# A row maximum over 64 MiB: the helper path for six rows goes, the loads are cut anew, and the first load comes as two transfers

## The chip, the cores and the metric

The kernel runs on one core of a Trainium2 chip. The metric is device time in microseconds (us) of one execution. Before the change three runs took 168.21, 168.44 and 169.49 us; the median is 168.44. One further view is the profile of one execution, whose span runs from its first to its last instruction.

## The reference

The input is float32 of shape 32 x 512 x 1024, drawn from a normal distribution; the output is the largest of the last 1024 elements:

```python
def reference(x):
    return np.max(x, axis=-1).astype(np.float32)
```

So there are 16,384 rows of 4,096 bytes, 67.1 MB to be read, and 64 KB to be written.

## The kernel before

The rows are laid over 128 partitions, 128 rows in each. They come in two blocks: 112 rows per partition, then 16. In a block, partition p holds consecutive rows of the input, so that a load of n rows per partition reads n x 4,096 consecutive bytes for each partition. `BLOCKS` lists the loads, as (n, m, w): n rows per partition are loaded, m of them go the helper path, and the result of these is folded in after load number w.

All loads are issued by SyncE (SP), in the order of the list, at L113. Their destination is a ring of 46 slots of 4,096 bytes per partition; a load takes n neighbouring slots and starts again at slot 0 where it would not fit. A load that takes used slots waits until the instructions that read them are done. The framework hands the loads eight semaphores in turn, so an issue can also wait for the landing of the load eight places back.

VectorE takes each load with one `reduce_max` (L124), which writes one value per row and partition into `res`. The last row of each partition is loaded as two halves (L134 into the ring, L135 into `tail`), reduced by L136 and L137; L137 takes the first half's result along with the second half.

Six rows per partition go another way (`by_gpsimd`): TensorE turns each row's 1024 columns in eight blocks of 128 x 128 into PSUM (L75), ScalarE copies them to SBUF (L81), GpSimd takes the maximum over the partitions (L83), TensorE turns one partition of that back in eight pieces of 128 x 1 (L88), and VectorE reduces the eight values per row (L95). `in_turn` holds the instructions of TensorE and of VectorE in the order in which they are written. The identity for the turns is made by GpSimd behind the first load (L121).

ScalarE issues two stores: the first block's results behind the last whole-row reduction (L140), the second block's at the end (L142).

## Time and profile before

| What | us |
|---|---|
| median of three runs | 168.44 |
| the profiled execution's own time | 169.49 |
| its span | 166.9 |
| VectorE (DVE) busy | 132.6 |
| TensorE (PE) busy | 16.6 |
| GpSimd (POOL) busy | 20.2 |
| ScalarE (ACT) busy | 7.4 |
| VectorE waits for loads, in total | 28.3 |
| VectorE waits for the turned-back rows (L95) | 3.5 |

In the profile, the slices are 40 equal parts of the span; a digit is the busy share in tenths. DVE is VectorE, DMA the mean share of the 16 transfer engines, and GB/s what they moved, counted where a packet starts. A line of the timeline has the start, the length, engine, line and operation, and in brackets how long the engine stood idle before and for whom. A row of the groups has the number of instructions, the total busy time, the mean length of one in ns, and the idle time ahead of them with what ended it. A row of the stretches has from and to, the length, each engine's busy time and count, the granted TensorE clock, the transfer engines' share and GB/s.

### The profile page before, as it was taken

What the parts mean: (1) busy time and instruction counts of PE and PEld (TensorE: products, weight loads), DVE (VectorE), ACT (ScalarE), POOL (GpSimd) and SP (SyncE); (2) the same over time, 40 slices, a digit from 0 to 9 for tenths busy, and PEclk for the clock granted to TensorE, in tenths of its full rate; (3) what the DMA queues carried; (4) which work ended last, traced back from release to release, by engine and by line L of the source; (5) the groups of instructions that cost most, each with busy time, mean ns of one, the idle gap of its engine ahead of it and who ended that gap; (6) DMA issues with size and microseconds to landing.
All of it is one profiled execution on the core that took longest, in us unless ns stands there. A gap on an engine that the chain in (4) does not pass through costs nothing.

```text
span 166.9 us, 329 instructions
## 1 busy us (share of the span) xinstructions
PE 16.6 (10%) x96; PEld 14.8 (9%) x96; DVE 132.6 (79%) x26; ACT 7.4 (4%) x7; POOL 20.2 (12%) x13
## 2 busy tenths in 40 slices
PE   0000000000000000000000000000008125382520
PEld 0000000000000000000000000000007125272420
DVE  0000089993999599986999999999999999999914
ACT  3000000000000000000000000000003100420200
POOL 0000000000000000000000000000002930777250
PEclk9999999999999999999999999999999855855555
DMA  6999879999979999989989999989999899999900
GB/s 236 471 471 471 383 324 471 471 471 412 442 324 471 471 457 427 442 348 495 412 389 415 433 512 400 464 384 442 461 389 440 385 457 404 418 405 411 392 15 16
DMA packets 3456, 67.18 MB, mean 403 GB/s; under 512 B 640, under 2 KB 640, under 8 KB 1792
## 3 DMA queue, kind: packets, MB, share of 16 engines
q1 hardware_dynamic: 3168, 67.11, 94.3%
q10 hardware_dynamic: 288, 0.07, 0.2%
HBM read 67.11 MB, written 0.07 MB: 403 GB/s over the span
## 4 chain that ended last, share of the span: by engine, by line
DMA 56%; DVE 29%; POOL 4%; PE 4%; issue 3%; POOLq 2%; ACT 1%; SPq 0%; ACTq 0%
DMA ring<-in_x_dram 56%; DVE res L124 28%; POOL top L83 4%; PE ps L75 2%; POOLq L168 2%; ACT sb L81 1%; PE back L88 1%; DVE res L137 0%; DVE tail L136 0%; SPq L113 0%; DVE res L95 0%; ACTq L81 0%
## 5 line engine op out<-in xcount | busy, mean ns | idle before, releaser
L124 DVE TENSOR_REDUCE res<-ring 128x1 f32<-128x1024 f32 (+7 forms) x20 | 131.3, 6599 | 28.4 <-DMA ring<-in_x_dram 28.3
L83 POOL PARTITION_ALL_REDUCE top<-sb x6 | 19.3, 3254 | 108.9 <-ACT sb L81 108.9
L75 PE MATMUL ps<-ident,ring 128*128 128x128 f32 x48 | 11.0, 418 | 129.1 <-DMA ring<-in_x_dram 129.1
L75 PEld LDWEIGHTS ps<-ident,ring 128*128 128x128 f32 x48 | 9.6, 224 | 129.1 <-issue 125.2
L81 ACT COPY sb<-ps 128x1024 f32<-128x1024 f32 x6 | 6.1, 1012 | 149.5 <-PE ps L75 149.5
L88 PE MATMUL back<-ident,top 1*128 1x1 f32 x48 | 5.7, 235 | 16.3 <-POOL top L83 16.3
L88 PEld LDWEIGHTS back<-ident,top 1*128 1x128 f32 x48 | 5.2, 201 | 17.9 <-POOL top L83 17.9
L95 DVE TENSOR_REDUCE res<-back 128x2 f32<-128x16 f32 (+1 forms) x4 | 0.6, 162 | 3.5 <-PE back L88 3.5
L121 POOL COPY ident<-ring 128x1 f32<-128x1 f32 x1 | 0.2, 188 | 21.1 <-DMA ring<-in_x_dram 21.1
masks.py:199 POOL TENSOR_SCALAR_AFFINE_SELECT ident<-ident 128x128 f32<-128x128 f32 x1 | 0.3, 282 | 10.5 <-issue 10.5
L81 ACT ACT_TABLE_LOAD x1 | 1.3, 1283 | 0.7 <-PEq L157 0.7
L137 DVE TENSOR_REDUCE res<-tail 128x1 f32<-128x513 f32 x1 | 0.7, 687 | 0.0
L136 DVE TENSOR_REDUCE tail<-ring 128x1 f32<-128x512 f32 x1 | 0.7, 674 | 0.0
masks.py:197 POOL MEMSET ident<- 128x128 f32 x1 | 0.2, 204 | 0.1
L157 POOL MEMSET const-float32-0.0<- 128x1 f32 x1 | 0.1, 98 | 0.2 <-issue 0.2
L157 POOL MEMSET const-uint8-127<- 128x1 uint8 x1 | 0.1, 102 | 0.0
L157 POOL MEMSET const-bfloat16-1.0<- 128x1 bf16 x1 | 0.1, 101 | 0.0
L157 POOL MEMSET const-float32-1.0<- 128x1 f32 x1 | 0.1, 98 | 0.0
## 6 DMA issues: line engine op xcount, KB each, us to landing
ring<-in_x_dram SPq DMA_DIRECT2D x4, 7680.0 KB, 39.0
ring<-in_x_dram SPq DMA_DIRECT2D x2, 3584.0 KB, 26.5
ring<-in_x_dram SPq DMA_DIRECT2D x1, 6144.0 KB, 34.7
ring<-in_x_dram SPq DMA_DIRECT2D x1, 5632.0 KB, 37.9
ring<-in_x_dram SPq DMA_DIRECT2D x1, 5120.0 KB, 32.3
ring<-in_x_dram SPq DMA_DIRECT2D x7, 512.0 KB, 21.1
ring<-in_x_dram SPq DMA_DIRECT2D x1, 2560.0 KB, 33.7
ring<-in_x_dram SPq DMA_DIRECT2D x1, 2048.0 KB, 38.1
```

What stands on the lines that cost most here:

```text
L75: in_turn("PE", nc.tensor.transpose(out=ps[:, c * P:(c + 1) * P], in_=rows[:, k, c * P:(c + 1) * P], identity=ident,))
L81: nc.scalar.copy(out=sb, in_=ps)
L83: nc.gpsimd.partition_all_reduce(top, sb, P, bass_isa.ReduceOp.max)
L88: in_turn("PE", nc.tensor.transpose(out=back[:, k, c:c + 1], in_=top[0:1, c * P:(c + 1) * P], identity=ident[0:1, 0:1],))
L95: return lambda: in_turn("DVE", nc.vector.reduce_max(out=cols, in_=back, axis=X))
L121: nc.gpsimd.tensor_copy(out=ident[:, 0:1], in_=xc[:, 0, 0:1])
L124: reduce = in_turn("DVE", nc.vector.reduce_max(out=cols[:, :n - m], in_=xc[:, :n - m, :], axis=X))
L136: in_turn("DVE", nc.vector.reduce_max(out=tail[:, PAD - 1:PAD], in_=half, axis=X))
L137: in_turn("DVE", nc.vector.reduce_max(out=res[:, I - 1:], in_=tail[:, PAD - 1:], axis=X))
L157: nc = _bacc.Bacc("TRN2", target_bir_lowering=False, num_devices=1)
L168: with _tile.TileContext(nc) as tc:
```

## The change

The helper path, with its pools, the identity and the order written out by hand, is taken out; VectorE reduces all rows. The two blocks still have 112 and 16 rows, but other loads: 15 and 12 of them, of falling size, instead of 10 and 10. The ring has 45 slots. The first load, of 14 rows, is issued as two transfers: partitions 0 to 15, then partitions 16 to 127; its reduction waits for both. The load of the first half of the last row starts again at slot 0 if there is no slot left.

```diff
 BLOCKS = [
-    [(15, 0, -1), (15, 0, -1), (15, 0, -1), (15, 0, -1), (12, 0, -1), (7, 0, -1), (11, 0, -1), (10, 2, 8), (7, 0, -1), (5, 2, 13)],
-    [(4, 1, 15), (2, 0, -1), (2, 1, 18), (1, 0, -1), (1, 0, -1), (1, 0, -1), (1, 0, -1), (1, 0, -1), (1, 0, -1), (1, 0, -1)],
+    [14, 13, 12, 11, 9, 8, 8, 7, 6, 5, 5, 4, 4, 3, 3],
+    [2, 2, 2, 1, 1, 1, 1, 1, 1, 1, 1, 1],
 ]
-RING = 46
+RING = 45
...
-        for n, m, w in loads:
+        for n in loads:
             if at + n > RING:
                 at = 0
             xc = ring[:, at:at + n, :]
-            nc.sync.dma_start(out=xc, in_=xb[:, b:b + n, :])
-            cols = res[:, first + b:first + b + n]
-            if m:
-                due.setdefault(w, []).append(by_gpsimd(xc[:, n - m:, :], cols[:, n - m:], m))
-            else:
-                run(backs)
-            if j == 0:
-
-                nc.gpsimd.tensor_copy(out=ident[:, 0:1], in_=xc[:, 0, 0:1])
-                make_identity(nc, ident)
-            if n > m:
-                reduce = in_turn("DVE", nc.vector.reduce_max(
-                    out=cols[:, :n - m], in_=xc[:, :n - m, :], axis=X))
-            run(due.get(j, []))
+
+            for p, q in ((0, 16), (16, P)) if first + b == 0 else ((0, P),):
+                nc.sync.dma_start(out=xc[p:q], in_=xb[p:q, b:b + n, :])
+            reduce = nc.vector.reduce_max(out=res[:, first + b:first + b + n], in_=xc, axis=X)
             at += n
             b += n
-            j += 1
         first += S
...
+    if at + 1 > RING:
+        at = 0
     half = ring[:, at, :H]
     nc.sync.dma_start(out=half, in_=xb[:, b, :H])
     nc.sync.dma_start(out=tail[:, PAD:], in_=xb[:, b, H:])
-    in_turn("DVE", nc.vector.reduce_max(out=tail[:, PAD - 1:PAD], in_=half, axis=X))
-    in_turn("DVE", nc.vector.reduce_max(out=res[:, I - 1:], in_=tail[:, PAD - 1:], axis=X))
+    nc.vector.reduce_max(out=tail[:, PAD - 1:PAD], in_=half, axis=X)
+    nc.vector.reduce_max(out=res[:, I - 1:], in_=tail[:, PAD - 1:], axis=X)
```

## The prediction

> **What bounds the kernel now.** I read the activity slices first, then the queue table and the timeline, because the question is whether the loads or VectorE carry the span.

> ```profile
> DVE  0000089993999599986999999999999999999914
> DMA  6999879999979999989989999989999899999900
> GB/s 236 471 471 471 383 324 471 471 471 412 442 324 471 471 457 427 442 348 495 412 389 415 433 512 400 464 384 442 461 389 440 385 457 404 418 405 411 392 15 16
> q1 hardware_dynamic: 3168, 67.11, 94.3%
> ```

> The transfer engines are full from the first slice to the last but two; the load queue alone takes 94.3% of 16 engines over the span. So the loads are a stream without holes, and whatever delays that stream early is still there at its end. The timeline gives its pace and its end:

> ```profile
> 21.45 16.15 DVE L124 TENSOR_REDUCE res<-ring 128x15 f32<-128x15360 f32 x1 [21.45 <-DMA ring<-in_x_dram]
> 58.44 16.15 DVE L124 TENSOR_REDUCE res<-ring 128x15 f32<-128x15360 f32 x1 [2.10 <-DMA ring<-in_x_dram]
> 76.59 48.33 DVE L124 TENSOR_REDUCE res<-ring 128x15 f32<-128x15360 f32 x4 [2.00 <-DMA ring<-in_x_dram]
> ...
> 149.57 0.33 SPq L134 DMA_DIRECT2D ring<-in_x_dram  x1
> ...
> 150.85 0.33 SPq L135 DMA_DIRECT2D tail<-in_x_dram  x1
> ...
> 161.97 0.17 DVE L95 TENSOR_REDUCE res<-back 128x1 f32<-128x8 f32 x1 [3.49 <-PE back L88]
> ...
> 163.89 0.69 DVE L137 TENSOR_REDUCE res<-tail 128x1 f32<-128x513 f32 x1
> ```

> Two loads of 15 rows lie 76.59 - 58.44 = 18.15 us apart. The issues of L134 and L135 each wait for the landing of a one-row load, so a one-row load takes 150.85 - 149.57 = 1.28 us. Both together: 1.205 us per row plus 0.075 us per transfer. The last load is issued at 150.85 and lands 8.9 us later (the table of issues), at 159.75. VectorE ends only at 164.58, since it stood 3.49 us before 161.97 waiting for the last row that TensorE, ScalarE and GpSimd reduce. The span ends 2.3 us later (the second store, 1.4 us to landing, and the end of the program).

> **The change, step by step.** The profiled execution took 169.49 us for its span of 166.9, so 2.6 lie around it; it is the slowest of the three runs, 1.05 over their median. I sum in its span and take the differences over to the median.

> Removed: six rows' path, 48 turns of 418 ns, six copies of 1.01 us, six all-reduces of 3.25 us, 48 turns back, four reductions of 0.16 us. All of it is on engines that the new kernel leaves idle, and only its end was on the path: the wait of 3.49. What is late next is the load stream itself and VectorE behind it.

> Added to VectorE: six rows. By shape the reductions are

> ```profile
> L124 DVE TENSOR_REDUCE res<-ring 128x15 f32<-128x15360 f32 x4 | 64.6, 16153 | 28.1 <-DMA ring<-in_x_dram 28.1
> L124 DVE TENSOR_REDUCE res<-ring 128x1 f32<-128x1024 f32 x8 | 9.5, 1211 | 0.1
> ```

> so (16153 - 1211) / 14 = 1067 ns per row; back to back each instruction costs about 70 ns more (five of them with 10 rows take 11.09). A row takes VectorE 1.07 us and the stream 1.205, so VectorE catches up wherever the next load isn't much shorter. The end is the largest of: a load's landing plus all reductions from it on. Row 112 landed at 139.7 before, with ten transfers (the 139.72 at which TensorE starts); with sixteen it is 139.7 + 6 x 0.075 = 140.15. Behind it: 3 rows 3.27, three times 2 rows 6.6, nine single rows 10.2, the two halves 1.3, together 21.4: 161.6. From the last landing: 159.75 + 8 x 0.075 = 160.35 (30 transfers for 22), plus 0.69 is 161.0. The other loads give at most 0.2 more than 161.6. I take 161.8, plus 2.3 = 164.1: **2.8 us less than 166.9**, as long as the stream runs as before.

> Issue and ring: each load's issue waits for the reductions whose slots it takes, and for the landing eight transfers back. Worked through by the same paces, SP issues load 4 at 35.3 (after reduction 1), where the stream has work until 50.5; load 6 at 63.4 against 74.7; the one-row loads about 9 us ahead. The smallest lead is 8.4 us, the way from issue to first packet is 1.0 to 2.1 us (issue 0.72; first packets below), so neither the waits nor the ring of 45 cost anything. One more issue of 0.33 us at the front lies beside the first packets.

> The split itself. What the first load does now, in stretches:

> ```profile
> 1.50:2.00 0.50, 0.00 (x0) 0.00 (x0) 0.00 (x0) 0.50 (x1) 0.00 (x0) 1.00 3.85 1229
> 2.00:2.50 0.50, 0.00 (x0) 0.00 (x0) 0.00 (x0) 0.00 (x0) 0.00 (x0) 1.00 1.71 614
> 2.50:3.00 0.50, 0.00 (x0) 0.00 (x0) 0.00 (x0) 0.00 (x0) 0.00 (x0) 1.00 0.28 123
> 3.00:4.00 1.00, 0.00 (x0) 0.00 (x0) 0.00 (x0) 0.00 (x0) 0.00 (x0) 1.00 0.00 0
> 4.00:6.00 2.00, 0.00 (x0) 0.00 (x0) 0.00 (x0) 0.00 (x0) 0.00 (x0) 1.00 1.13 492
> ```

> The last column counts a packet where it starts; a packet is one partition's 15 rows, 61,440 bytes. 1229 GB/s over 0.5 us are ten packets, then five, then one: each of 16 engines starts one between 1.5 and 3.0, and the next 16 start after 4. An engine therefore sends its eight partitions one after another, 18.15 / 8 = 2.27 us each, 27 GB/s. What could be won by an earlier start is the spread of these starts, 0 to 1.0 us.

> What could be lost: now the first packet of all 16 engines goes into 16 neighbouring partitions, 57,344 bytes each, 2.12 us at full pace. No row shows such a transfer. Eight partitions that one engine serves are never seen to take more than 27 GB/s together. If this is a limit of the memory's side (a group of eight partitions behind one entrance), 16 neighbours lie in 2 to 16 groups: in 16 the transfer takes 2.1 us, in 8 4.2, in 4 8.5, in 2 16.9. I take 8.5, the middle step on the slow side, because the pace per engine never rises above 27 in any stretch, as an entrance's limit would have it, and because neighbours are likelier to share than to be spread out: **6.3 us lost** (0 to 14.8; or a gain of up to 1.0). The engines can't pass it: each has its later packets behind its first.

> The second transfer: 112 partitions, seven packets per engine, 14.8 us at full pace. An engine's share is now seven partitions, not the eight of a group, so two engines meet in one group. Best under the same limit: the busiest group must take its eight packets, 16.9 us. Worst: two engines together all the way, 29.6. I take 22.4, the middle in ratio: **7.6 us lost** (2.1 to 14.8). Where the limit doesn't exist, nothing is lost here either. Later loads go as before, but an engine that is behind stays behind, since the stream has no hole to catch up in: 6.3 + 7.6 = 13.9 on every later landing, thus on the end.

> Sum: -2.8 + 13.9 = 11.1 more: 166.9 + 11.1 = 178.0 of span, 180.6 for such an execution, **179.5** against the median of 168.44.

> [...]

> **The rivals.** (a) No shared entrance, the engines' own pace is the only limit: the sum stops at -2.8, less up to 1.0 for the earlier start: 165.6 (164.6 to 166.5), *faster* than before. For it: 27 GB/s per engine is just as well an engine's limit. The turning point: the split must lose less than 2.8 us. The same time comes out if a partition belongs to a fixed engine, so that the first piece goes through a few engines and the second fills up the rest: then the change doesn't do what it says. (b) Only the first piece is held up, or it goes four packets deep on four engines (three more at 2.1 each, 6.3): 165.6 + 6.3 = 171.9. Against (b): the first piece's limit would have to vanish for the second. (c) Both pieces at the slow end: 165.6 + 29.6 = 195.2. Against it: it needs all 16 partitions in two groups.

> **Chances.** The forecast (first piece 8.5, second anywhere from 16.9 to 29.6: 174.0 to 186.7) 0.58; (b) 0.22; (c) and beyond 186.7 0.05; (a) 0.13; between (a) and (b), 0.02. The range from 171 to 187 holds the first two, 8 in 10; the forecast's own is 174 to 187. A measurement of this kernel can tell about 1% from no change: below 166.8 only (a), so faster 0.13, the same 0.02, slower 0.85.

> **What would show it.** In the new profile, right: packets that start by 2 us and none of the second transfer until about 10; VectorE's first reduction (14 rows) starting near 34 instead of 20.2, its wait on the loads that much longer; later landings of the 13 and 12 rows 15.7 and 14.5 us apart, as fast as before; VectorE ending within 2 us of the last landing, with no TensorE or GpSimd in the chain. Wrong: a first reduction at 20 (then (a)) or near 26.5 (then (b)); holes in the stream at 35 or 50 would mean a late issue, which I priced at nothing; a pace other than 1.205 us per row later would mean that the engines don't stay apart as I think.

## The result, and the profile after

The changed kernel takes 183.71 us (median of six runs, 183.31 to 184.32), the kernel before 169.38 (six runs): 1.086 times as long, 95% interval 1.082 to 1.091. Forecast were 179.5, within 171 to 187.

Three rows of the changed kernel's page, its span in 40 slices:

```profile
DVE  0000000049989998999999999999999999999994
DMA  9279989989899989999999999999999999999980
GB/s 202 50 151 315 290 202 214 318 351 433 386 480 389 476 377 476 436 388 462 389 463 425 389 454 420 429 429 423 423 432 434 425 421 430 413 416 412 406 326 16
```

Read the two transfer rows together. The share of busy engines is as high as before in nearly every slice (a packet's time, like its bytes, is counted where it starts, hence the 2 in the second slice), but in the first eight slices, 36 us, the engines move 50 to 318 GB/s, where the kernel before moved 236 in its first slice and 324 to 471 in the next seven. They aren't idle, they are slow; after that they go as before (351 to 480 GB/s in the ninth to the 38th slice, where the kernel before has 324 to 512). VectorE starts in the ninth slice instead of the sixth. The timeline gives the times:

```profile
38.98 15.09 DVE L60 TENSOR_REDUCE res<-ring 128x14 f32<-128x14336 f32 x1 [38.98 <-DMA ring<-in_x_dram]
54.63 14.02 DVE L60 TENSOR_REDUCE res<-ring 128x13 f32<-128x13312 f32 x1 [0.57 <-DMA ring<-in_x_dram]
69.16 12.95 DVE L60 TENSOR_REDUCE res<-ring 128x12 f32<-128x12288 f32 x1 [0.51 <-DMA ring<-in_x_dram]
...
112.84 65.46 DVE L60 TENSOR_REDUCE res<-ring 128x8 f32<-128x8192 f32 x21 [0.21 <-DMA ring<-in_x_dram]
...
169.33 0.33 SPq L70 DMA_DIRECT2D tail<-in_x_dram  x1
...
178.92 0.69 DVE L72 TENSOR_REDUCE res<-tail 128x1 f32<-128x513 f32 x1
```

The first reduction starts at 38.98, where the kernel before had 21.45. The next ones follow 15.65 and 14.53 us later, the forecast's 15.7 and 14.5: the stream has its old pace again. The tail half lands at 169.33 + 8.9 = 178.2, and VectorE ends at 179.61, 1.4 us behind it. Nothing that was lost at the start is won back: VectorE still waits for a load ahead of 112.84, and from there on it works without a pause. The stretches of the start (the last column is GB/s, counted where a packet starts):

```profile
1.50:2.00 0.50, 0.00 (x0) 0.00 (x0) 1.00 11.31 1376
2.00:2.50 0.50, 0.00 (x0) 0.00 (x0) 1.00 1.75 229
2.50:3.00 0.50, 0.00 (x0) 0.00 (x0) 1.00 1.81 229
3.00:4.00 1.00, 0.00 (x0) 0.00 (x0) 1.00 0.00 0
4.00:6.00 2.00, 0.00 (x0) 0.00 (x0) 1.00 0.00 0
6.00:8.00 2.00, 0.00 (x0) 0.00 (x0) 1.00 0.00 0
8.00:10.00 2.00, 0.00 (x0) 0.00 (x0) 1.00 1.92 373
```

Twelve, two and two packets of 57,344 bytes: the sixteen of the first piece. Then no packet starts until after 8 us. By the packets in the trace these sixteen take 6.8 to 8.2 us each, where the later packets of the same load take 2.12 in the kernel with one transfer, 27 GB/s per engine (called full pace below); the last ends at 10.15. The 112 packets of the second piece then take about 4 us each (the medians of the seven rounds are 4.6, 4.1, 2.8, 3.2, 3.9, 4.0 and 3.9), and the last ends at 38.12.

### The profile page after: what moved, and what is told of

It reads as the page before. It is cut to its first block, busy times and chain, and to the rows that moved or that the text cites. A ratio compares the mean times of both kernels' runs of the same rounds, so it can differ in the third digit from the quotient of the medians.

```text
span 181.9 us, 119 instructions
## 1 busy us (share of the span) xinstructions
DVE 138.9 (76%) x29; POOL 0.2 (0%) x4
## 3 DMA queue, kind: packets, MB, share of 16 engines
q1 hardware_dynamic: 4192, 67.11, 96.5%
HBM read 67.11 MB, written 0.07 MB: 369 GB/s over the span
## 4 chain that ended last, share of the span: by engine, by line
DVE 60%; DMA 37%; another core or an unknown queue 1%; SPq 0%; issue 0%; DVEq 0%
DVE res L60 59%; DMA ring<-in_x_dram 37%; SPq L59 0%; DVE res L72 0%; DVE tail L71 0%; DVEq L60 0%
## 5 line engine op out<-in xcount | busy, mean ns | idle before, releaser
L60 DVE TENSOR_REDUCE res<-ring 128x1 f32<-128x1024 f32 (+12 forms) x27 | 137.7, 5165 | 40.6 <-DMA ring<-in_x_dram 40.6
## 6 DMA issues: line engine op xcount, KB each, us to landing
ring<-in_x_dram SPq DMA_DIRECT2D x1, 5632.0 KB, 28.4
```

The costliest lines, as they stand in the source:

```text
L60: reduce = nc.vector.reduce_max(out=res[:, first + b:first + b + n], in_=xc, axis=X)
```

## The experiments

**One transfer instead of two.**

```diff
-            for p, q in ((0, 16), (16, P)) if first + b == 0 else ((0, P),):
+            for p, q in ((0, P),):
```

> The new kernel with its first load as one transfer of 128 partitions. Theory E (16 neighbouring partitions share a few entrances of the memory, each limited to what one engine gives): the loss goes entirely, first reduction at 20.2 us instead of 39.0, median 2.8 us below the kernel before, ratio 0.983. Theory S (the falling loads and the missing helper path cost the time, not the split): still about 14 us above the kernel before, ratio about 1.08.

Measured: 164.96 us, ratio to the kernel before 0.975 (0.972 to 0.979). The timeline:

```profile
20.29 15.09 DVE L60 TENSOR_REDUCE res<-ring 128x14 f32<-128x14336 f32 x1 [20.29 <-DMA ring<-in_x_dram]
36.04 14.02 DVE L60 TENSOR_REDUCE res<-ring 128x13 f32<-128x13312 f32 x1 [0.66 <-DMA ring<-in_x_dram]
...
94.23 65.47 DVE L60 TENSOR_REDUCE res<-ring 128x8 f32<-128x8192 f32 x21 [0.21 <-DMA ring<-in_x_dram]
...
160.33 0.69 DVE L72 TENSOR_REDUCE res<-tail 128x1 f32<-128x513 f32 x1
```

The first reduction comes 18.7 us earlier than in the changed kernel, the end of VectorE 18.6, the time 18.75. So the split costs 18.7 us, and all the rest of the change saves 4.4 (164.96 against 169.38).

**The split alone, in the kernel before.** Its issue at L113 becomes the two transfers.

```diff
-            nc.sync.dma_start(out=xc, in_=xb[:, b:b + n, :])
+            for p, q in ((0, 16), (16, P)) if first + b == 0 else ((0, P),):
+                nc.sync.dma_start(out=xc[p:q], in_=xb[p:q, b:b + n, :])
```

> The kernel before with only its first load (15 rows) split into partitions 0 to 15 and 16 to 127. Theory E: first packets of 7 to 9 us, then seven of about 4.3 us; the first reduction 18.7 x 15/14 = 20 us later than 21.4, and the end 18 to 20 us later, 187 to 189. Theory S: within 1 us of the kernel before.

Measured: 188.27 us, ratio 1.112 (1.107 to 1.117), 18.9 us more. L125 is the L124 of the kernel before:

```profile
42.03 16.15 DVE L125 TENSOR_REDUCE res<-ring 128x15 f32<-128x15360 f32 x1 [42.03 <-DMA ring<-in_x_dram]
60.10 16.15 DVE L125 TENSOR_REDUCE res<-ring 128x15 f32<-128x15360 f32 x1 [1.92 <-DMA ring<-in_x_dram]
```

The first reduction starts at 42.03 instead of 21.45, 20.6 later, and VectorE ends at 184.37 instead of 164.58, 19.8 later. The loss doesn't need the new schedule.

**Two transfers, cut by rows.** All 128 partitions in both.

```diff
-            for p, q in ((0, 16), (16, P)) if first + b == 0 else ((0, P),):
-                nc.sync.dma_start(out=xc[p:q], in_=xb[p:q, b:b + n, :])
+            for r, s in ((0, 1), (1, n)) if first + b == 0 else ((0, n),):
+                nc.sync.dma_start(out=xc[:, r:s], in_=xb[:, b + r:b + s, :])
```

> The new kernel with its first load in two transfers again, but cut by rows: one row for all 128 partitions, then 13 rows. Theory E: as the kernel with one transfer, 0.1 us more for one more transfer, first reduction at 20.3, ratio 0.983. Theory T (two transfers at the start cost the time, whatever they hold): first reduction near 39, about 14 us above the kernel before.

Measured: 164.94 us, first reduction at 20.29, the same as with one transfer. It isn't the number of transfers.

**A cut in the middle.**

```diff
-((0, 16), (16, P))
+((0, 64), (64, P))
```

> The changed kernel with its first load cut at partition 64 instead of 16. Theory E, by the sets measured alone (18.6 us for partitions 0 to 63, 18.5 for 64 to 127, of which some 0.7 each is start): first reduction at about 39, the time within 1.5 us of the changed kernel, 182 to 185. If it were the small first piece that costs: near the kernel with one first transfer, 165.

Measured: 183.95 us in one run, first reduction at 39.11. Two pieces of 64 partitions cost the same as 16 and 112, so it isn't the smallness of the first piece. The two come to the same total by different steps: here each of the eight packets of an engine takes about 4.5 us, there the first takes 6.8 to 8.2 and the others about 4.

**A small first load, split.**

```diff
-    [14, 13, 12, 11, 9, 8, 8, 7, 6, 5, 5, 4, 4, 3, 3],
+    [1, 14, 13, 12, 11, 9, 8, 8, 7, 6, 5, 5, 4, 4, 3, 2],
```

> The changed kernel with a first load of one row ahead of the 14 rows (the last load of the first block has 2 rows instead of 3); only that one row is split at partition 16. Theory E: the loss goes with the bytes that are split, 18.7 / 14 = 1.3 us, so 166.4. Theory T (the loss comes from splitting whatever the size): near 183.

Measured: 166.06 us, ratio to the kernel before 0.980 (0.974 to 0.986). That is 1.1 above the kernel with one transfer, or 1.4 when each is taken against the kernel before as measured beside it (169.05 here, 169.38 there). Two more transfers explain 0.15 of it, at the 0.075 us each that the prediction worked out. So the loss isn't one of splitting as such; at this one size it fits a loss that goes with the bytes that come in the split way.

**Sets of partitions, each by itself.** The last three kernels are the one with one first transfer; behind its last issue they load 14 rows into one set of partitions after another, and each load waits for the one ahead. Each was executed once; the loads of all 128 partitions among them, eight in all, took 18.0 to 18.4 us. The list of the first of them, as (from, to, step):

```diff
+PROBES = [(0, 128, 1), (0, 16, 1), (0, 32, 1), (0, 64, 1), (0, 112, 1), (16, 128, 1), (64, 128, 1), (0, 128, 1), (16, 48, 1), (32, 128, 1), (0, 128, 8), (0, 64, 4), (0, 128, 1)]
...
+    n = BLOCKS[0][0]
+    xb = xf[:views_rows * P, :].rearrange("(p i) d -> p i d", p=P)
+    for p, q, s in PROBES:
+        nc.sync.dma_start(out=ring[p:q:s, :n, :], in_=xb[p:q:s, :n, :])
```

> The new kernel with one first transfer, and behind its last issue 13 further loads of 14 rows, each waiting for the landing of the one ahead, into different sets of partitions; its time is longer by these loads and is not compared. From first packet's start to last packet's end, theory E with groups as four neighbours and the four 32 further on: all 128: 17; 0-15: 8.5; 0-31: 8.5; 0-63: 17; 64-127: 17; 16-47: 8.5; 16 partitions eight apart (0, 8, .. 120): 4.2; 16 partitions four apart (0, 4, .. 60): 4.2; 0-111 and 16-127: the same as each other, 17 to 30; 32-127: 13 to 26. Theory P (an engine's own pace is the only limit, the slow start of the new kernel being a matter of the first microseconds): 2.1 us for each of an engine's packets: 17, 2.1, 4.2, 8.5, 8.5, 4.2, 2.1, 2.1, 14.8, 14.8, 12.7.

The shape of theory E's groups was the author's assumption: no run before this one shows it.

The stretches of this run, each cut to one load: all 128 partitions, 0 to 15, 0 to 31, 0 to 63, 0 to 111, 16 to 127, 64 to 127. The last column is GB/s.

```profile
161.00:179.20 18.20, 0.00 (x0) 0.00 (x0) 1.00 0.97 404
180.40:189.10 8.70, 0.00 (x0) 0.00 (x0) 1.00 0.84 105
190.80:200.70 9.90, 0.00 (x0) 0.00 (x0) 1.00 0.87 185
202.30:221.00 18.70, 0.00 (x0) 0.00 (x0) 1.00 0.94 196
222.40:250.50 28.10, 0.00 (x0) 0.00 (x0) 1.00 0.95 229
251.80:280.30 28.50, 0.00 (x0) 0.00 (x0) 1.00 0.92 225
282.10:300.70 18.60, 0.00 (x0) 0.00 (x0) 1.00 0.95 197
```

**Smaller sets.**

> The new kernel with one first transfer, and behind its last issue 12 further loads of 14 rows (57,344 bytes a partition, 2.12 us at an engine's full pace), one at a time; its time is not compared. From first packet's start to the last end, plus up to 0.7 for the start. Theory G (a group is four neighbours and the four 32 further on; 64 further on is another group): partitions 0-3: 8.5; 0,4,8,12: 2.1; 0-7: 8.5; 0 and 32: 4.2; 0 and 64: 2.1; 0 and 4: 2.1; 0,4,..28: 2.1; 0,32,64,96: 4.2; 32 partitions four apart: 8.5. Theory N (a group is eight neighbours): 8.5; 4.2; 17; 2.1; 2.1; 4.2; 4.2; 2.1; 4.2. One more set is for the second transfer: 16 partitions seven apart, as its 16 engines start. By G 14 groups are met, twelve once and two twice: twelve packets near 2.1 and four near 4.2. Theory H (whatever isn't the complete set of 128 goes at half pace at best): all sixteen near 4.2, and 0 and 64 or 0,4,8,12 at 4.2 too.

The stretches of three pairs, 0 and 32, 0 and 64, and 0 and 4:

```profile
212.50:217.10 4.60, 0.00 (x0) 0.00 (x0) 1.00 0.12 25
219.20:222.70 3.50, 0.00 (x0) 0.00 (x0) 1.00 0.11 33
224.30:227.70 3.40, 0.00 (x0) 0.00 (x0) 1.00 0.12 34
```

Measured, from first start to last end: 0-3: 7.6; 0, 4, 8, 12: 3.1; 0-7: 7.8; 0 and 32: 4.5; 0 and 64: 3.4; 0 and 4: 3.3; 0, 4, .. 28: 3.1; 0, 32, 64, 96: 4.4; 32 partitions four apart: 5.3. A first packet in the loads of all 128 partitions takes 2.1 to 3.5 us, so 3.1 to 3.4 is taken as full pace; 4.4 to 4.5 is about half pace (2 x 2.12 = 4.24). These times fit theory G in eight of nine: 0 and 32 (4.5) go as in one group, 0 and 64 (3.4) and 0 and 4 (3.3) as in two. N fails at 0-7, at 0 and 32, and at 0, 32, 64, 96. The ninth went better than G said: all 16 second packets of the 32 partitions took 2.12 us, so, if the groups are G's, the engines were not handed the partitions in order here. Which engine gets which partition isn't recorded. The set seven apart fitted neither G nor H: its packets took 2.6 to 4.4 us, most of them between 3.2 and 3.9.

**Sets in the middle.**

> The new kernel with one first transfer, and behind its last issue 11 further loads of 14 rows, one at a time; its time is not compared. They ask why the second transfer took 28 us, near the slow end. Theory G (a group: four neighbours and the four 32 further on; sets of 16 to 112 are handed to the engines in order, an engine that shares a group with another goes at half pace, one that doesn't at full pace), with up to 0.7 for the start: partitions 32-95, 16 fours of 16 different groups, 8.5 (0-63 took 18.6); 32, 36, .. 92: 2.1 (0, 4, .. 60 took 4.8); 64, 68, .. 92: 2.1; 48-111: eight engines finish at 8.5 and eight at 16.9; 48, 52, .. 108: eight packets near 2.1 and eight near 4.2; 40, 44, .. 100: twelve near 2.1, four near 4.2; 16-111: 21. Theory C (where some engines share a group, all slow down): 32-95 as by G, but 48-111 with hardly a packet of 2.1 and all engines ending near 17, 48, 52, .. 108 and 40, 44, .. 100 with most packets between 2.8 and 4.4, 16-111 at 25 or more. Theory H (all but the complete set at half pace): 17, 4.2, 2.1, 17, 4.2, 4.2, 25.

A four is here four neighbouring partitions, the first a multiple of four. The stretches of partitions 32 to 95, of 32, 36, .. 92, of 48 to 111, of 48, 52, .. 108, of 40, 44, .. 100, and of 16 to 111:

```profile
181.00:190.40 9.40, 0.00 (x0) 0.00 (x0) 1.00 0.96 390
192.00:195.40 3.40, 0.00 (x0) 0.00 (x0) 1.00 0.81 270
197.00:215.10 18.10, 0.00 (x0) 0.00 (x0) 1.00 0.91 190
217.00:221.70 4.70, 0.00 (x0) 0.00 (x0) 1.00 0.88 195
...
248.00:252.70 4.70, 0.00 (x0) 0.00 (x0) 1.00 0.86 195
...
274.60:301.50 26.90, 0.00 (x0) 0.00 (x0) 1.00 0.94 200
```

Partitions 32 to 95 come at 390 GB/s, nearly as fast as all 128 (404) and twice as fast as 0 to 63: the same number of partitions, bytes and packets, but by theory G 16 groups instead of eight. H is out. In 48 to 111, half of the engines should have a group to themselves by G; yet the first packets take 3.5 to 4.5 us, all later ones about 4.48, and the whole takes 18.1. Partitions 40 to 103, where by G four of the sixteen fours share, take 18.15. The sets of single partitions need no guess on which engine has which: all sixteen packets run at once (in 40, 44, .. 100 the sixteen engines are busy for 0.86 of the 4.7 us), so each is alone on its engine. In 40, 44, .. 100, no packet takes less than 3.6 although by G only four of the sixteen share; in 48, 52, .. 108, none less than 3.7; in 32, 36, .. 92, where by G none share, they take 2.2 to 3.1. These times fit theory C: in the sets where some share, the others were slow with them. The 26.9 us of 16 to 111, where G gave 21 and C 25 or more, fit it. Why an engine that by G shares with nobody was slow wasn't settled.

In all these loads partition p is filled from the p-th equal piece of the input (`xb`), so the partitions written and the addresses read change together. The runs show that the time goes with the set; they don't show whether the groups belong to the partitions or to the addresses.

## Why the prediction was right, point by point

**The stream as the bound, and a late start that stays.** Right: the delay of the first reduction (18.7), of VectorE's end (18.6) and of the time (18.75) are one number to within 0.2 us.

**The first piece.** Taken at 8.5 us, 6.3 lost. By itself it took 8.5; in the kernel its last packet ended at 10.15, against 5.14 for the first sixteen packets of the kernel with one transfer: 5.0 lost, since the first packets of that kernel too need up to 3.3 us, and this start adds nothing visible to the shared ones. The ground, groups with a limit of about one engine's pace, fits the sets: 0 to 3 came at 30 GB/s (7.6 us), where one engine gives 27. So does the step "four groups" among two to sixteen: 0 to 15, four fours, came at 108 GB/s (8.5 us), and 0, 4, 8, 12, one of each four, at full pace (3.1 us). The rows before the change didn't give that step, though: the prediction chose it as the middle on the slow side. That was luck as far as its own rows go. That the groups go by the partitions, and not by the addresses, was not shown.

**The second piece.** The mis-sized term: taken at 22.4 us between 16.9 and 29.6, 7.6 lost. Measured were 28.4 by itself, and 38.12 - 10.15 = 28.0 in the kernel, where one transfer needed 14.8: 13.2 lost. So the first reduction came at 38.98 and not near 34. The slow end of the range was nearly right and its ground was not: by the sets in the middle it isn't that every engine meets another all the way, but that all engines were slow where some meet (40, 44, .. 100: no packet under 3.6 us). Which engine has which partition in this piece isn't recorded, so for the kernel itself that is inferred.

**The rest of the change.** Taken at -2.8, measured -4.4. Of the difference of 1.6, half lies in the span: the last landing is at 150.71 + 9.0 = 159.7 in the kernel with one transfer, not 160.35, and VectorE's end at 161.02, not 161.8. The forecast had built on the landings of the one profiled execution before, where the slowest transfer engine fell from 0.5 to 1.2 us behind the fastest between 36 and 40 us; in the kernel with one transfer the distance stays at 0.6 until 120 us, and then shrinks with the packets. The other half lies around the span: 1.8 us (165.12 for a span of 163.3) instead of 2.6. The split in the kernel before bears on both, since that kernel keeps the helper path: in its four runs 1.7 to 1.8 us lie around the span, where seven runs of the kernel before beside it have 2.0 to 2.8, and its second reduction follows the first by 18.07 us, where the kernel before has 18.74. These two make most of the way from its 20.6 us at the first reduction to 19.8 at VectorE's end and 18.9 in the time. So the helper path alone doesn't cause the part around the span, and hardly the other; what does is open. The waits, the ring and the additional transfers cost next to nothing, as was said: with one first transfer the span is 163.3 us, shorter than the forecast's 164.1, not longer.

**The sum.** -2.8 + 6.3 + 7.6 = 11.1 forecast; -4.4 + 18.7 = 14.3 measured. Of the 18.7, 5.0 are the first piece, 13.2 the second, and 0.5 lie between the last packet's end and the first reduction (0.86 us with the split, 0.36 with one transfer), which the prediction didn't have. The direction and the likeliest case were right. The largest error, 5.6 us in the second piece, was offset by half through 1.3 in the first piece and 1.6 in the rest of the change; that the time came as near as it did is partly luck.

**The rivals.** (a), no shared entrance, fell with the set of 0 to 63 (18.6 us, where the engines' own pace gives 8.5), and with its time: it would be the kernel with one transfer. (b) fell with the first reduction at 38.98, where it had 26.5, and with 16 to 127 at 28.4 us by themselves. (c) needed two groups, 16.9 us for the first piece, which took 8.5 by itself, the time for four; its second piece, at the slow end, came nearly true.

**The earlier start.** Bounded at 0 to 1.0 us, and nothing came: in the half us after 1.5, twelve packets started with the split and thirteen without it.

The kernel with one first transfer, at 164.96 us, beats both the kernel before and the changed one; cutting it by rows (164.94) neither helps nor hurts.

## What to carry to other kernels

Before splitting a transfer by partitions, time the set of each piece by itself, for sets of one size can differ; here 64 partitions' worth of bytes took 9.4 us for 32 to 95 and 18.6 for 0 to 63. Where a load stream is full from end to end, cut it by rows and keep all 128 partitions in each transfer, which was faster here (164.94 us, against 183.71 and 183.95 for the cuts at partitions 16 and 64). A row of busy transfer engines says little by itself: read the GB/s beneath it (in the seventh slice 9 tenths at 214 GB/s with the split, and 9 tenths at 471 in the kernel before).

## What the runs showed of the hardware that was not expected

- The slow pace wasn't confined to the packets that share. Sixteen packets on sixteen groups by G (32, 36, .. 92) took 2.2 to 3.1 us each; with four of the sixteen in shared groups by G (40, 44, .. 100), no packet took less than 3.6.
- 32 partitions four apart (0, 4, .. 124) came at full pace, 5.3 us for two packets per engine, the second ones 2.12 each, where handing them to the engines in order would put pairs of engines into one group, if the groups are G's.
- In loads of 128 partitions behind a pause, the first packets take 2.1 to 3.5 us, in the median 2.8, where later ones take 2.12: the start cost about 0.7 us there.
